# Gate and up products of the latent tokens as seven half-size products (Strassen's algorithm) in a two-layer diffusion trunk

## The chip, the core and the metric

One core of a Trainium2 chip runs the whole kernel in one launch. The metric is the device time of an execution in microseconds, as the median of several runs.

## What is computed

The reference is a trunk of two layers over 1024 latent tokens and 256 context tokens of width 1024, in float32. Each layer has a mixer (gated linear attention, spatial gating, windowed attention, one output projection) and a SwiGLU feed-forward block, both between norms and with modulation:

```
y = concat(a, b, c) @ w_out                     # mixer output
x = x + mod[2] * rmsnorm(y, n1_post)
h = modulate(rmsnorm(x, n2_pre), mod[3], mod[4])
g, u = split(h @ w_gu, 2)                       # w_gu 1024 x 5632
f = (silu(g) * u) @ w_down                      # w_down 2816 x 1024
x = x + mod[5] * rmsnorm(f, n2_post)
```

The last layer computes the feed-forward block for the latent tokens alone. The modulation vectors are `silu(c) @ mod_w + mod_b`, six of 1024 for each layer and each of the two streams of tokens.

## The kernel before, in words

Tokens stand in ten tiles of 128: tiles 0 and 1 are context, 2 to 9 latent. Every matrix product is done with both operands split into a high part (a cast to fp32r) and a low part, the rest. `mm3` (L179) issues three matmuls for one product: high x high, high x low, low x high. A split of something that lies in SBUF is a cast on ScalarE and a subtraction on VectorE; `split` (L164) does this for a weight: a load by SP into one of two staging tiles `ws`, the cast (L172), the subtraction (L173).

`ffn` (L1096) runs everything after the mixer of a layer. It goes over the tokens in two halves, `HALVES`: five tiles each in layer 0, four each in layer 1. For each half the output projection runs first: `cat_tile` transposes the mixer's output, and `down_group` (L972, matmuls at L984) multiplies a tile by four weight slices at a time, with pairs of 512-column matmuls into two PSUM banks, and collects the sums in `yas`. `post` (L1001) norms, gates and adds the residual; `normed` and `modulate` (L403, transposes at L400) make the transposed input of the feed-forward block, split into `hh` and `hl`.

Then, per half, the 22 chunks of 128 hidden units. `ahead` splits the gate and up weights of a chunk before they are needed. `product` (L1151) computes for a chunk and a stretch of tokens the gate and the up product, each over 8 slices of 128 of the model's width and each with three matmuls; ScalarE takes SiLU of the gate out of PSUM, VectorE multiplies by the up product, and the result is split into `gh` and `gl`. In layer 0 a half of 640 tokens is done in two stretches of 320 columns (384 and 256 in the first group), in layer 1 a half is one stretch of 512. After every four chunks `down_group` adds their part of the down-projection to `yas`. All weights of gate, up and down are therefore loaded and split once for each half.

In layer 0 a second generator, `mod_stream` with "dve", is merged with `ffn`: seven pieces of modulation vectors, each 16 loads of 128x512 into a ring `ms` of two tiles, and for each load two VectorE operations (L376 for the first of a sum, L378 for the rest) that add a row of the weights times a scalar into `macc`. `merge` takes from each generator in proportion to its planned total (here 840 units for `ffn`, 105 for the sums), and the order in which the program text is recorded is, with a scheduler's look-ahead, the order on each engine.

Of the kernel before, what the change touches and what calls it, by code (L numbers as in the profile page):

```python
# [16 lines left out]
D = 1024  # L17
# [104 lines left out]

class Net:
# [55 lines left out]
    def mm3(self, out, ah, al, bh, bl, first, last):  # L179
        mm = self.nc.tensor.matmul  # L180
        mm(out, ah, bh, start=first, stop=False)  # L181
        mm(out, ah, bl, start=False, stop=False)  # L182
        mm(out, al, bh, start=False, stop=last)  # L183
# [859 lines left out]
    def layer(self, l):  # L1043
# [3 lines left out]
        with tp("ss", "left") as sp_:  # L1047
# [41 lines left out]
        with tp("ff", "left") as fp:  # L1089
            streams = [(420.0 * (2 if need_ctx else 1.6), self.ffn(l, fp, need_ctx))]  # L1090
            if l + 1 < self.layers:
                streams.append((MOD_SHARE_FFN, self.mod_stream("dve", [(0, 5)] + [(l + 1, j) for j in (1, 0, 2, 3, 4, 5)])))
                self.mring = fp, 2
            merge(*streams)

    def ffn(self, l, fp, need_ctx):  # L1096
        nc, a = self.nc, self.a
        halves = [list(range(*x)) for x in (HALVES if need_ctx else ((CT, 6), (6, TT)))]
        G = 4
        hh, hl = self.H  # L1100
        WO, WG, WD = a["w_out"], a["ffn_w_gu"], a["ffn_w_down"]
        row = lambda w, k: w[l, k * P : (k + 1) * P, :]
        seconds = dict(tags=("dh", "dl"), pool=fp)

        def cat_tile(slot, i):
            pv = self.turned(self.cat[i], None)
            s = slice(slot * P, (slot + 1) * P)
            nc.scalar.copy(hh[:, :, s], pv)
            nc.vector.tensor_sub(hl[:, :, s], pv, hh[:, :, s].bitcast(F32))

        def cats(tiles):
            return [lambda slot=slot, i=i: cat_tile(slot, i) for slot, i in enumerate(tiles)]

        queue = [c for _ in halves for c in range(NFC)]
        ready = []

        def ahead():
            if queue:
                c = queue.pop(0)
                ready.append([self.split(self.cols(WG, l, 0, KC, f * FF + c * P, f * FF + (c + 1) * P), D) for f in range(2)])  # L1120

        early = cats(halves[0])
        for f in early[:2]:
            f()
        with self.tc.high_priority(offset=400):
            w0 = [self.split(row(WO, k), D) for k in range(4)]
        for f in early[2:]:
            f()
        w1 = [self.split(row(WO, k), D, **seconds) for k in range(4, 8)]
        gates = self.gates(l, 2, fp, need_ctx)  # L1130
        yas = [self.t(fp, f"ya{t_}", [P, D]) for t_ in range(5)]
        norm2 = [self.normed(2 * l + 1, lambda i: self.x1[l][i], tiles, l, 3) for tiles in halves]
        for hi, tiles in enumerate(halves):
            done = lambda ti, i: self.post(fp, i, yas[ti], gates, self.x_src(l, i), self.x1[l][i], self.ss[2 * l + 1], False, not need_ctx)
            yield from self.down_group([hh[:, k, :] for k in range(4)], [hl[:, k, :] for k in range(4)], w0, tiles, yas, True, None, None)
            if hi == 0:
                w0 = [self.split(row(WO, k), D) for k in range(4)]
            else:
                ahead()
            yield from self.down_group([hh[:, k, :] for k in range(4, 8)], [hl[:, k, :] for k in range(4, 8)], w1, tiles, yas, False, done,  # L1140
                                       cats(halves[1]) if hi == 0 else norm2[0])
            if hi == 0:
                w1 = [self.split(row(WO, k), D, **seconds) for k in range(4, 8)]
        groups = [range(0, NFC % G)] + [range(c, c + G) for c in range(NFC % G, NFC, G)]
        final = l == self.layers - 1
        for hi, tiles in enumerate(halves):
            n = len(tiles) * P
            for gi, cs in enumerate(groups):
                ghs, gls, wts = [], [], []

                def product(pair, ci, p0, p1):  # L1151
                    s, sz = slice(p0, p1), p1 - p0
                    ps = self.b2()
                    for wi, (wh, wl) in enumerate(pair):
                        for k in range(KC):
                            ks = slice(k * P, (k + 1) * P)
                            self.mm3(ps[:, wi * 512 : wi * 512 + sz], wh[:, ks], wl[:, ks], hh[:, k, s], hl[:, k, s], k == 0, k == KC - 1)
                    sg = self.t(fp, "sg", [P, 512], bufs=2)[:, :sz]
                    self.act(sg, ps[:, :sz], AF.Silu)
                    nc.vector.tensor_mul(sg, sg, ps[:, 512 : 512 + sz])  # L1160
                    nc.scalar.copy(ghs[ci][:, s], sg)
                    nc.vector.tensor_sub(gls[ci][:, s], sg, ghs[ci][:, s].bitcast(F32))
                    return 6.5 * sz / 320

                def begin():
                    pair = ready.pop(0)
                    for x, o in (("gh", ghs), ("gl", gls)):
                        o.append(self.t(fp, x, [P, 640], F32R, bufs=5))
                    return pair

                if gi == 0:

                    pairs = [begin()]
                    ahead()
                    pairs.append(begin())
                    for ci in range(2):
                        yield product(pairs[ci], ci, 0, n - 256)
                    wts.append(self.split(row(WD, cs[0]), D, **seconds))
                    yield product(pairs[0], 0, n - 256, n)
                    ahead()  # L1180
                    wts.append(self.split(row(WD, cs[1]), D, **seconds))
                    yield product(pairs[1], 1, n - 256, n)
                else:
                    parts = 2 if n > 512 else 1
                    for ci, c in enumerate(cs):
                        pair = begin()
                        ahead()
                        for p_ in range(parts):
                            yield product(pair, ci, p_ * n // parts, (p_ + 1) * n // parts)
# [146 lines left out]
```

## Time and profile before

| | |
|---|---|
| median of 3 runs | 2998.67 us (2994.62 to 3002.09) |
| profiled execution, its own time | 2993.22 us |
| its span | 2991.4 us |
| mean granted clock of TensorE | 0.978 |
| feed-forward part of layer 0, from the out-projection's first matmul to the last of the down-projection | 627.0 to 1688.2 us |
| the same of layer 1, to the end of the span | 2156.5 to 2991.4 us |

The profile is that of one execution. Busy time is the time in which an engine worked on an instruction; matmuls overlap their neighbours, so that the mean length of one is more than the distance from one start to the next, and their ends are modelled. Times in the timeline are counted from the span's start.

### The profile page before, as it was taken

Reading aid. Unit: us, or ns where it says so; the run is one execution under the profiler, and the core shown is the slowest. Engines: PE = TensorE matmul, PEld = TensorE weight load, DVE = VectorE, ACT = ScalarE, POOL = GpSimd, SP = SyncE. Lnnn points to the kernel's source line nnn. Section 1 sums busy time; section 2 is a strip of 40 time slices with the busy share of each in tenths; the row PEclk is TensorE's granted clock in tenths of the full one; section 3 lists DMA queues with packets and bytes.
Section 4 is the critical chain, followed back from the end, with each engine's and each line's share of the span. In section 5 each row is a group of like instructions: output and inputs, shape, how many; then the busy total and the mean of one; then the engine's idle time right before and its main releaser. Section 6 shows DMA issues by size and latency. Waiting matters only on the chain. (4 is left out here: it accounts for less than half of the span.)

```text
span 2991.4 us, 45447 instructions
## 1 busy us (share of the span) xinstructions
PE 2883.5 (96%) x18072; PEld 2570.9 (86%) x18072; DVE 1750.9 (59%) x3586; ACT 1220.2 (41%) x2426; POOL 209.2 (7%) x172
## 2 busy tenths in 40 slices
PE   6999899989999999999999999899799999999998
PEld 4899788878999999999999899888688888888887
DVE  3465577878866533885333685688776333553334
ACT  4453576644422222522222464577554222342222
POOL 0000233300000000000000000233200000000000
PEclk8999799989999999999999999999899999999999
DMA  8743000076644322553222453100465332353232
GB/s 242 216 142 90 24 12 8 22 245 204 198 131 152 106 85 83 182 166 106 85 71 73 126 147 92 57 9 12 140 212 170 101 102 87 101 160 101 89 92 78
DMA packets 347393, 338.05 MB, mean 113 GB/s; under 512 B 42528, under 2 KB 284460, under 8 KB 347180
## 3 DMA queue, kind: packets, MB, share of 16 engines
q1 hardware_dynamic: 344924, 329.37, 36.0%
q0 software_dynamic: 1536, 3.15, 0.4%
q8 instruction: 142, 2.33, 0.3%
q10 hardware_dynamic: 720, 2.62, 0.2%
q14 instruction: 71, 0.58, 0.1%
HBM read 304.38 MB, written 30.70 MB: 112 GB/s over the span
## 5 line engine op out<-in xcount | busy, mean ns | idle before, releaser
L181 PE MATMUL b<-hh,wh 128*128 128x320 f32 (+3 forms) x2648 | 870.9, 329 | 4.2 <-DVE ht L411 3.0
L182 PE MATMUL b<-hl,wh 128*128 128x320 f32 (+3 forms) x2648 | 868.2, 328 | 0.0
L183 PE MATMUL b<-hh,wl 128*128 128x320 f32 (+3 forms) x2648 | 868.0, 328 | 0.0
L181 PEld LDWEIGHTS b<-hh,wh 128*128 128x128 f32 x2648 | 498.4, 188 | 35.3 <-DVE ht L411 3.9
L182 PEld LDWEIGHTS b<-hl,wh 128*128 128x128 f32 x2648 | 498.3, 188 | 26.6 <-issue 0.8
L183 PEld LDWEIGHTS b<-hh,wl 128*128 128x128 f32 x2648 | 498.3, 188 | 25.3
L173 DVE TENSOR_TENSOR wl<-ws,wh 128x1024 fp32r<-128x1024 f32 x192 | 234.6, 1224 | 412.1 <-ACT wh L172 411.8
L172 ACT CAST wh<-ws 128x1024 fp32r<-128x1024 f32 x192 | 201.2, 1050 | 475.0 <-PE b L182 352.1
L172 ACT CAST dh<-ws 128x1024 fp32r<-128x1024 f32 x104 | 108.9, 1047 | 348.1 <-PE b L984 270.3
L984 PE MATMUL b<-dh,gh 128*128 128x512 f32 x792 | 246.2, 391 | 0.2 <-ACT ya L989 0.2
L984 PE MATMUL b<-dl,gh 128*128 128x512 f32 x792 | 244.9, 390 | 0.5 <-DVE dl L173 0.5
L991 DVE TENSOR_TENSOR ya<-ya,b 128x512 f32<-128x512 f32 x216 | 139.5, 682 | 180.9 <-PE b L984 180.8
L984 PE MATMUL b<-dh,gl 128*128 128x512 f32 x792 | 244.6, 390 | 0.0
L181 PE MATMUL b<-wh,hh 128*128 128x256 f32 (+1 forms) x592 | 173.2, 294 | 8.2 <-DVE hh L413 3.8
L984 PEld LDWEIGHTS b<-dl,gh 128*128 128x128 f32 x792 | 148.5, 188 | 32.4 <-DVE dl L173 1.6
L984 PEld LDWEIGHTS b<-dh,gl 128*128 128x128 f32 x792 | 148.7, 188 | 31.2
L984 PEld LDWEIGHTS b<-dh,gh 128*128 128x128 f32 x792 | 147.1, 188 | 30.5 <-ACT ya L989 0.9
L183 PE MATMUL b<-wh,hl 128*128 128x256 f32 (+1 forms) x592 | 171.0, 289 | 1.2 <-DVE hl L414 1.2
L182 PE MATMUL b<-wl,hh 128*128 128x256 f32 (+1 forms) x592 | 171.5, 290 | 0.3 <-DVE wl L487 0.3
L487 DVE TENSOR_TENSOR wl<-ws,wh 128x1024 fp32r<-128x1024 f32 (+2 forms) x68 | 79.8, 1176 | 152.7 <-ACT wh L486 152.7
L173 DVE TENSOR_TENSOR dl<-ws,dh 128x1024 fp32r<-128x1024 f32 x104 | 127.1, 1222 | 62.9 <-ACT dh L172 62.4
L378 DVE SCALAR_TENSOR_TENSOR macc<-ms,csil,macc 128x512 f32<-128x512 f32 x196 | 139.5, 746 | 37.0 <-DMA ms<-in_mod_w 36.5
(257 smaller groups left out, 4682.3 us busy)
## 6 DMA issues: line engine op xcount, KB each, us to landing
ws<-in_ffn_w_gu SPq DMA_DIRECT2D x176, 512.0 KB, 3.9
ws<-in_ffn_w_down SPq DMA_DIRECT2D x88, 512.0 KB, 3.6
ms<-in_mod_w SPq DMA_DIRECT2D x144, 256.0 KB, 3.0
ws<-in_w_in SPq DMA_DIRECT2D x56, 512.0 KB, 4.3
ws<-in_w_out SPq DMA_DIRECT2D x32, 512.0 KB, 4.6
xt<-cat SPq DMA_DIRECT2D x18, 512.0 KB, 4.6
xt<-x SPq DMA_DIRECT2D x18, 512.0 KB, 3.6
xp<-x SPq DMA_DIRECT2D x18, 512.0 KB, 4.7
```

The source lines that it names most:

```text
L172: nc.scalar.copy(h[:, :width], sv)
L173: nc.vector.tensor_sub(l[:, :width], sv, h[:, :width].bitcast(F32))
L181: mm(out, ah, bh, start=first, stop=False)
L182: mm(out, ah, bl, start=False, stop=False)
L183: mm(out, al, bh, start=False, stop=last)
L378: nc.vector.scalar_tensor_tensor(x, st, c, x, op0=ALU.mult, op1=ALU.add)
L487: nc.vector.tensor_sub(lo[:, : kk * nn], st[:, : kk * nn], h[:, : kk * nn].bitcast(F32))
L984: nc.tensor.matmul(ps[n], x[:, s], y[:, n * 512 : (n + 1) * 512], start=(c == 0 and pi == 0), stop=(c == nk - 1 and pi == 2))
L991: nc.vector.tensor_add(y, y, ps[n])
```

## The change

The gate and up product of the latent tokens is a product of a 1024 x 1024 activation matrix with, for each chunk, a 1024 x 256 weight matrix (128 gate columns and 128 up columns). The new class `Up` cuts it in two by two blocks: tokens 2 to 5 and 6 to 9 (`a1.`, `a2.`), first and second half of the width (`a.1`, `a.2`; `b1.`, `b2.`), gate and up (`b.1`, `b.2`). In place of eight block products it does seven, of 4 slices x 3 matmuls x 512 columns each, of sums of blocks: `t1` to `t4` are made of the weights, `s1` to `s4` of the activations. A chunk now serves all latent tokens at once. GpSimd computes the four weight differences of a chunk (`diff`) and the two products of gate and up; ScalarE copies three partial results out of PSUM and VectorE makes three sums that read PSUM; seven weight blocks are split per chunk (`prepare`, by `halve`), each 128x512, into slots that exist once. The results go to DRAM (`gd`, DMAs issued by GpSimd).

Around it the stages are laid out anew. `mix_out` does the output projection of all tiles with all eight weight slices resident, post and norm one and two tiles behind, and the sums of activations (VectorE and GpSimd; `s3`, `s4` and `a22` through DRAM); the norm's root goes by table. Then the stream of chunks, in layer 0 merged with the modulation sums (418 to 105 units). `up_context` then computes gate and up of the 256 context tokens with ordinary products, for which it loads `w_gu` a second time. `down_stage` runs the down-projection as before with `down_group`, from activations re-read from DRAM and split again; the down weights are still loaded once for each half.

```diff
+class Up:
+    DIFFS = {"t1": ("b12", "b11"), "t2": ("b22", "t1"), "t3": ("b22", "b12"), "t4": ("b21", "t2")}
...
+    def load(self, c):
+        for f in range(2):
+            t = self.stage(f).rearrange("p (k n) -> p k n", k=KC)
+            self.nc.sync.dma_start(t, self.net.cols(self.net.a["ffn_w_gu"], self.l, 0, KC, f * FF + c * P, f * FF + (c + 1) * P))
+            self.raw[c, f"b1{f + 1}"], self.raw[c, f"b2{f + 1}"] = t[:, 0:4], t[:, 4:8]
...
+    def diff(self, c, x):
+        p, q = self.DIFFS[x]
+        v = self.raw[c, x] = self.net.t(self.gp, "tt", [P, 4, P], bufs=3)
+        self.nc.gpsimd.tensor_sub(v, self.raw[c, p], self.raw[c, q])
+
+    def prepare(self, c, x):
+        self.net.halve(*self.slot(c, x), self.raw[c, x])
...
+    def chunk(self, c):
+        nc, net, n = self.nc, self.net, c + 1
+        more = n < NFC
+        xz, Y = net.b2(), net.b1()
+        X, Z = xz[:, :512], xz[:, 512:]
+        store = lambda at, t: nc.gpsimd.dma_start(self.gd[c][:, at : at + 512], t)
+        self.product(X, c, "b11", "a11", True)
+        p1 = self.tmp()
+        nc.scalar.copy(p1, X)
+        self.product(Y, c, "b21", "a12", True)
+        g0 = self.tmp()
+        nc.vector.tensor_add(g0, Y, p1)
+        net.act(g0, g0, AF.Silu)
+        yield 5.4
+        if more:
+            self.load(n)
+        self.product(X, c, "t2", "s2")
+        u2 = self.tmp()
+        nc.scalar.copy(u2, X)
+        self.product(Z, c, "t1", "s1", True)
+        p5 = self.tmp()
+        nc.scalar.copy(p5, Z)
+        if more:
+            self.prepare(n, "b11")
+            self.prepare(n, "b21")
+            self.diff(n, "t1")
+            self.diff(n, "t2")
+        yield 5.4
+        self.product(X, c, "t3", "s3")
+        c22 = self.tmp()
+        nc.vector.tensor_add(c22, X, p5)
+        if more:
+            self.prepare(n, "t1")
+            self.prepare(n, "t2")
+        yield 2.7
+        self.product(Z, c, "b22", "s4")
+        c12 = self.tmp()
+        nc.vector.tensor_add(c12, Z, u2)
+        nc.gpsimd.tensor_mul(g0, g0, c12)
+        store(256, g0)
+        if more:
+            self.diff(n, "t3")
+            self.prepare(n, "b22")
+            self.prepare(n, "t3")
+        yield 2.7
+        self.product(X, c, "t4", "a22")
+        g1 = self.tmp()
+        net.act(g1, X, AF.Silu)
+        nc.gpsimd.tensor_mul(g1, g1, c22)
+        store(768, g1)
+        if more:
+            self.diff(n, "t4")
+            self.prepare(n, "t4")
+        yield 2.7
...
+            with tp("cx", "left") as cx:
+                streams = [(NFC * 19.0, st)]
+                if l + 1 < self.layers:
+                    streams.append((MOD_SHARE_FFN, self.mod_stream("dve", [(0, 5)] + [(l + 1, j) for j in (1, 0, 2, 3, 4, 5)])))
+                    self.mring = cx, 2
+                merge(*streams)
...
+    def mix_out(self, l, px, A, up, tp):
...
+        for n, i in enumerate(order):
+            product(i)
+            if n + 2 < len(order):
+                cat(order[n + 2])
+            if n:
+                post(order[n - 1])
+                residual(i)
+            if n > 1:
+                norm(order[n - 2])
+            if n == len(order) - 3:
+                up.load(0)
+                up.prepare(0, "b11")
+                up.prepare(0, "b21")
...
+    def halve(self, h, lo, v):
+
+        self.nc.scalar.copy(h, v)
+        self.nc.vector.tensor_sub(lo, v, h.bitcast(F32))
```

Three places show how instructions stand now. On GpSimd, behind the last work of layer 0's mixer, there was nothing until the mixer of layer 1 (`ao`, `cat` and `sink` belong to the mixers, `uv` to layer 1's):

```order
L827 TENSOR_TENSOR ao_7017<-v_484,gld_7014 128x256 [waits DMAHW3_49,DMAHW5_49,DVE_49,Pool_49]
L827 TENSOR_TENSOR ao_7023<-v_484,gld_7020 128x256 [waits DMAHW4_49,DMAHW6_49,DVE_49,Pool_49]
L950 DMA cat_84<-co_6358 128x512 [waits DVE_49]
L1261 TENSOR_SCALAR sink_16687<-sink_16687 128x8 [waits DMAHW6_49,DVE_49,PE_49]
L1248 DMA uv_18596<-in_gdi 128x2x512 [waits DMAHW0_49,DMASW2_49,DMAHW1_49,DMASW1_49,DMAHW2_49,DMASW0_49,DMAHW3_49,DVE_49,DMAHW7_49,PE_49,Activation_49]
```

Now a chunk of the stream puts six operations and two stores there (`ct` are the temporaries of `chunk`, `tt` the differences t1, t2, t3, t4 in this order, `ru` and `rg` the loaded weights of up and gate):

```order
L230 TENSOR_TENSOR ct_9086<-ct_9086,ct_9190 128x512 [waits DVE_49]
L197 DMA gd_0_7114<-ct_9086 128x512 [waits DMASW2_49,Pool_49]
L240 TENSOR_TENSOR ct_9216<-ct_9216,ct_9155 128x512 [waits DMASW1_49,Activation_49]
L173 TENSOR_TENSOR tt_9305<-ru_9267,rg_9265 128x512 [waits DMAHW4_49,DMAHW0_49]
L197 DMA gd_0_7114<-ct_9216 128x512 [waits Pool_49]
L173 TENSOR_TENSOR tt_9307<-ru_9267,tt_9305 128x512 [waits Pool_49]
L173 TENSOR_TENSOR tt_9363<-ru_9267 128x512 [waits DVE_49]
L173 TENSOR_TENSOR tt_9389<-rg_9265,tt_9307 128x512 [waits DVE_49,Pool_49]
```

The first difference of a chunk stands behind the last product of the chunk before, and the last difference frees `rg` for its next load.

On VectorE, in layer 0's feed-forward part, the sums (`macc`) stood between halvings of weights and of results:

```order
L378 SCALAR_TENSOR_TENSOR macc_10416<-ms_10727,csil_150,macc_10416 128x512 [waits DMAHW2_49,DVE_49]
L378 SCALAR_TENSOR_TENSOR macc_10416<-ms_10727,csil_150,macc_10416 128x512 [waits DVE_49]
L173 TENSOR_TENSOR wl_9587<-ws_9584,wh_9586 128x1024 [waits PE_49,Activation_49]
L378 SCALAR_TENSOR_TENSOR macc_10416<-ms_10759,csil_150,macc_10416 128x512 [waits DMAHW3_49,DVE_49]
L378 SCALAR_TENSOR_TENSOR macc_10416<-ms_10759,csil_150,macc_10416 128x512 [waits DVE_49]
L378 SCALAR_TENSOR_TENSOR macc_10416<-ms_10819,csil_150,macc_10416 128x512 [waits DMAHW4_49,DVE_49]
L1160 TENSOR_TENSOR sg_9567<-sg_9567,b_1665_9518 128x320 [waits Activation_49]
L173 TENSOR_TENSOR wl_9593<-ws_9590,wh_9592 128x1024 [waits DMAHW5_49]
L1162 TENSOR_TENSOR gl_9443<-sg_9567,gh_9442 128x320 [waits Activation_49]
```

Now they stand between the halvings of the seven blocks (`t1l` is not shown, `t3l`, `b11l`, `b21l`, `b22l` are) and the sums L222 and L229 that empty PSUM:

```order
L503 SCALAR_TENSOR_TENSOR macc_10037<-ms_10173,csil_150,macc_10037 128x512 [waits DMAHW2_49,DVE_49]
L503 SCALAR_TENSOR_TENSOR macc_10037<-ms_10173,csil_150,macc_10037 128x512 [waits DVE_49]
L503 SCALAR_TENSOR_TENSOR macc_10037<-ms_10181,csil_150,macc_10037 128x512 [waits DMAHW3_49,DVE_49]
L503 SCALAR_TENSOR_TENSOR macc_10037<-ms_10181,csil_150,macc_10037 128x512 [waits DVE_49]
L222 TENSOR_TENSOR ct_9677<-b_1801_9578,ct_9647 128x512 [waits PE_49,Activation_49]
L1384 TENSOR_TENSOR t3l_9714<-tt_9707,t3h_9713 128x512 [waits Activation_49]
L1384 TENSOR_TENSOR b11l_9820<-rg_9787,b11h_9819 128x512 [waits DMAHW4_49,Activation_49]
L1384 TENSOR_TENSOR b21l_9824<-rg_9787,b21h_9823 128x512 [waits PE_49,Activation_49]
L503 SCALAR_TENSOR_TENSOR macc_10037<-ms_10233,csil_150,macc_10037 128x512 [waits DMAHW5_49,DVE_49]
L503 SCALAR_TENSOR_TENSOR macc_10037<-ms_10233,csil_150,macc_10037 128x512 [waits DVE_49]
L229 TENSOR_TENSOR ct_9703<-b_1801_9578,ct_9633 128x512 [waits DMASW4_49,PE_49]
L1384 TENSOR_TENSOR b22l_9710<-ru_9619,b22h_9709 128x512 [waits Activation_49]
```

The two sums that read PSUM wait for TensorE and stand in one row with everything else; the halving of `b21` of a chunk two ahead stands before the sum L229.

On TensorE, at the end of a chunk (`b_1801` holds its X and Z, `b_1875` the Y of the chunk two ahead), this is the row; before, all matmuls of a chunk and a stretch stood together:

```order
L305 MATMUL b_1801_9578<-s4h_8426,b22l_9541 128x512
L305 MATMUL b_1875_9918<-a12h_7105,b21h_9823 128x512 [waits Activation_49]
L305 MATMUL b_1875_9918<-a12l_7106,b21h_9823 128x512
L305 MATMUL b_1875_9918<-a12h_7105,b21l_9824 128x512 [waits DVE_49]
L305 MATMUL b_1875_9918<-a12h_7105,b21h_9823 128x512
L305 MATMUL b_1875_9918<-a12l_7106,b21h_9823 128x512
L305 MATMUL b_1875_9918<-a12h_7105,b21l_9824 128x512
L305 MATMUL b_1875_9918<-a12h_7105,b21h_9823 128x512
L305 MATMUL b_1801_9578<-a22h_8428,t4h_9570 128x512 [waits DVE_49]
L305 MATMUL b_1801_9578<-a22l_8429,t4h_9570 128x512
```

The second product of the chunk two ahead (with `b21h`, `b21l`) begins in front of the chunk's last product (with `t4h`), and the latter waits for VectorE's sum L222.

## Rows read from the trace of the kernel before

**Rows 1.** The page's first part: busy time, share of the span, instructions of each engine.
```profile
PE 2883.5 (96%) x18072; PEld 2570.9 (86%) x18072; DVE 1750.9 (59%) x3586; ACT 1220.2 (41%) x2426; POOL 209.2 (7%) x172
```

**Rows 2.** Busy time by stretch: length, engines with instructions, clock, DMA share, GB/s.
```profile
680.00:720.00 40.00, 38.86 (x177) 31.55 (x176) 36.06 (x91) 22.37 (x35) 0.00 (x0) 1.00 0.76 256
1200.00:1400.00 200.00, 200.00 (x1232) 189.00 (x1231) 156.76 (x283) 70.32 (x124) 0.00 (x0) 1.00 0.52 163
2400.00:2600.00 200.00, 200.00 (x888) 165.54 (x886) 75.60 (x88) 50.98 (x61) 0.00 (x0) 1.00 0.33 98
```

**Rows 3.** TensorE's timeline, three places: start, length, instruction; 320, 512 and 256 columns.
```profile
999.88 0.31 PE L181 MATMUL b<-hh,wh 128*128 128x320 f32 x1
...
1002.08 0.31 PE L181 MATMUL b<-hh,wh 128*128 128x320 f32 x1
...
2420.80 0.39 PE L181 MATMUL b<-hh,wh 128*128 128x512 f32 x1
...
2425.33 0.39 PE L183 MATMUL b<-hh,wl 128*128 128x512 f32 x1
...
250.10 0.28 PE L181 MATMUL b<-wh,hh 128*128 128x256 f32 x1
...
253.94 0.28 PE L183 MATMUL b<-wh,hl 128*128 128x256 f32 x1
```

**Rows 4.** TensorE's timeline, layer 0's gate and up product begins; idle before in brackets.
```profile
753.02 0.44 PE L181 MATMUL b<-hh,wh 128*128 128x384 f32 x1 [2.29 <-DVE ht L411]
...
756.45 0.48 PE L183 MATMUL b<-hh,wl 128*128 128x384 f32 x1
756.77 0.34 PE L181 MATMUL b<-hh,wh 128*128 128x384 f32 x1
756.94 0.33 PE L182 MATMUL b<-hl,wh 128*128 128x384 f32 x1
```

**Rows 5.** SP's timeline, the out-projection's weights in layer 0.
```profile
628.43 1.47 SPq L169 DMA_DIRECT2D ws<-in_w_out  x2
...
635.16 2.83 SPq L169 DMA_DIRECT2D ws<-in_w_out  x2
```

**Rows 6.** Groups by form: line, engine, operation, count, busy us, mean ns, idle before.
```profile
L173 DVE TENSOR_TENSOR wl<-ws,wh 128x1024 fp32r<-128x1024 f32 x192 | 234.6, 1224 | 412.1 <-ACT wh L172 411.8
L172 ACT CAST wh<-ws 128x1024 fp32r<-128x1024 f32 x192 | 201.2, 1050 | 475.0 <-PE b L182 352.1 <-DMA ws<-in_ffn_w_gu 96.4 <-DMA ws<-in_w_out 21.1
...
L378 DVE SCALAR_TENSOR_TENSOR macc<-ms,csil,macc 128x512 f32<-128x512 f32 x196 | 139.5, 746 | 37.0 <-DMA ms<-in_mod_w 36.5
...
L1162 DVE TENSOR_TENSOR gl<-sg,gh 128x512 fp32r<-128x512 f32 x40 | 27.5, 686 | 7.6 <-ACT gh L1161 7.6
...
L154 ACT ACTIVATE sg<-b 128x512 f32<-128x512 f32 x40 | 23.5, 588 | 13.0 <-PE b L183 13.0
```

**Rows 7.** The page's DMA issues: count, KB each, median us from issue to landing.
```profile
ws<-in_ffn_w_gu SPq DMA_DIRECT2D x176, 512.0 KB, 3.9
```

**Rows 8.** Timelines of VectorE and GpSimd in layer 0's mixer, 404 to 416.
```profile
406.63 0.69 DVE L909 TENSOR_TENSOR ptl<-b,pth 128x512 fp32r<-128x512 f32 x1 [1.40 <-ACT pth L908]
...
405.64 2.37 POOL L737 TENSOR_TENSOR qk<-qk,ep 128x1024 f32<-128x1024 f32 x1 [12.70 <-ACT ep L154]
...
411.46 1.28 POOL L749 TENSOR_TENSOR lv<-el,k 128x512 f32<-128x512 f32 x1 [1.12 <-ACT el L154]
```

**Rows 9.** VectorE's timeline in layer 0's feed-forward stage: two neighbours.
```profile
1254.39 0.74 DVE L378 SCALAR_TENSOR_TENSOR macc<-ms,csil,macc 128x512 f32<-128x512 f32 x1
1255.05 1.22 DVE L173 TENSOR_TENSOR wl<-ws,wh 128x1024 fp32r<-128x1024 f32 x1
```

**Rows 10.** Timelines of VectorE and GpSimd in layer 0's mixer, 338 to 350.
```profile
340.70 3.73 DVE L862 TENSOR_TENSOR qs<-sq,qs 64x512 fp32r<-64x512 f32 x2
...
340.09 2.12 POOL L734 TENSOR_TENSOR qk<-q,k 128x1024 f32<-128x1024 f32 x1 [2.32 <-PE b L757]
342.17 1.71 POOL L749 TENSOR_TENSOR lv<-el,k 128x512 f32<-128x512 f32 x1
```

More of the change, by code (lines that the diff above doesn't have):

```diff
@@ L177, in cols, with mm3 @@
         return w[l, k0 * P : k1 * P, c0:c1].rearrange("(k p) n -> p k n", p=P)
[L179 to L183, printed above, removed]
+    def mm3(self, out, ah, al, bh, bl, first, last, more=False):
+        mm = lambda x, y, **kw: self.nc.tensor.matmul(out, x, y, skip_group_check=more, **kw)
+        mm(ah, bh, start=first, stop=False)
+        mm(ah, bl, start=False, stop=False)
+        mm(al, bh, start=False, stop=last)
     def rstd(self, ss, n, scale, eps, out=None):
@@ L1087, in layer @@
                 merge(*streams)
-        self.open_hp()
[L1089 to L1096, printed above, removed]
+        with tp("fa", "left") as fa:
+            A = {x + p: self.t(fa, x + p, [P, 4, 512], F32R) for x in ("a11", "a12", "s2", "s1") for p in "hl"}
+            up = Up(self, l, fa, A)
+            with tp("px", "left") as px:
+                rest = self.mix_out(l, px, A, up, tp)
+                next(rest)
+                st = up.stream()
+                next(st)
+                for _ in rest:
+                    pass
+            with tp("cx", "left") as cx:
[4 more added lines that the diff above has]
+                merge(*streams)
+            up.close()
@@ L1111, in cats @@
[L1111 to L1123, printed above, removed]
-            f()
-        with self.tc.high_priority(offset=400):
-            w0 = [self.split(row(WO, k), D) for k in range(4)]
@@ L1127, in ffn @@
[L1127 to L1189, printed above, removed]
-                        wts.append(self.split(row(WD, c), D, **seconds))
-                last = gi == len(groups) - 1
-                nxt = None
-                if last and hi + 1 < len(halves):
-                    nxt = norm2[hi + 1]
-                elif last and not final:
-                    nxt = self.normed(2 * l + 2, lambda i: self.x_src(l + 1, i), range(5), l + 1, 0)
-                    self.plan(l + 1)
-                if last and hi == 0:
-                    gates = self.gates(l, 5, fp, need_ctx)
-                done = lambda ti, i: self.post(fp, i, yas[ti], gates, self.x1[l][i], self.x_dst(l, i),
-                                               self.ss[2 * l + 2] if need_ctx else None, final and hi == 1, not need_ctx)
-                yield from self.down_group(ghs, gls, wts, tiles, yas, gi == 0, done if last else None, nxt)
@@ new lines, in down_stage, with fetch @@
+        sizes = [[2, 4, 4, 4, 4, 4], [4, 3, 3, 3, 3, 3, 3]]
+        work = []
+        for hi in range(2):
+            c = 0
+            for n in sizes[hi]:
+                work.append((hi, range(c, c + n)))
+                c += n
+        def fetch():
+            if not work:
+                return None
+            hi, cs = work.pop(0)
+            g, w = [], []
+            for c in cs:
+                w.append(weight(c))
+                g.append(acts(c, halves[hi]))
+            loads[0] += 1
+            return hi, cs, g, w
@@ new lines, in down_stage @@
+        cur = fetch()
+        yas = [self.t(dn, f"ya{t_}", [P, D]) for t_ in range(5)]
+        gates = self.gates(l, 5, dn, need_ctx)
+        nxt = []
+        if not final:
+            nxt = self.normed(2 * l + 2, lambda i: self.x_src(l + 1, i), range(5), l + 1, 0)
+        while cur:
+            ahead = fetch()
+            hi, cs, g, w = cur
+            tiles = halves[hi]
+            last = cs.stop == NFC
+            done = lambda ti, i: self.post(dn, i, yas[ti], gates, self.x1[l][i], self.x_dst(l, i),
+                                           self.ss[2 * l + 2] if need_ctx else None, final and hi == 1, not need_ctx)
+            for _ in self.down_group([x for x, _ in g], [x for _, x in g], w, tiles, yas, cs.start == 0, done if last else None, None):
+                pass
+            if hi == 1 and cs.start and nxt:
+                nxt.pop(0)()
+                if len(nxt) == 1:
+                    self.plan(l + 1)
+            cur = ahead
@@ L1204, in x_dst @@
+        for f in nxt:
+            f()
     def x_dst(self, l, i):
```

215 lines of the change are left out of this document (205 added, 10 removed).

## The prediction

> **What bounds the kernel now.** I read the page's first part, then busy time by stretch, then start times on TensorE, then its waits. TensorE is busy for 2883.5 of 2991.4 us [rows 1]. In the feed-forward stretches it has no hole: 200.00 of 200 us from 1200 to 1400 and from 2400 to 2600, at granted clock 1.00, that is 2.4 GHz, while the DMA share is 0.52 and 0.33 [rows 2]. So each matmul less there is worth its start-to-start time, not its busy time, which overlaps the next one's. These steps are 0.1467 us for 320 columns (15 of them from 999.88 to 1002.08), 0.2265 for 512 (20 from 2420.80) and 0.120 for 256 (32 from 250.10) [rows 3]. VectorE is busy 157 and 76 us of 200 in these stretches, GpSimd not at all [rows 2]: the change takes its time from engines that seem to have room, and for each I ask whether the room is enough.
>
> **What is removed.** Layer 0: 22 chunks x 2 matrices x 8 slices x 3 products = 1056 groups, each 4 matmuls of 320 columns on average over the two halves, so 4224 x 0.1467 = 619.7 us. After: 22 x 7 products x 12 = 1848 matmuls of 512 columns, 418.6 us, and for the 256 context tokens, which keep eight products, 1056 of 256 columns, 126.7 us: 74.4 us less. Layer 1: 2112 x 0.2265 = 478.4 us become 418.6: 59.8 us less. Out-projection and down-projection keep their columns. Together **-134.2 us**. The old stages lose little that could be won back: from 680 to 720 TensorE misses 1.1 us [rows 2]; at 753.02 it waits 2.29 us for the normed tile, then the 384-column matmuls start 0.32 us apart until 756.5, then 0.17, as at 1.2 and 2.4 GHz, which costs another 1.6 [rows 4]. With as much for layer 1, I give **-8 us**.
>
> **What is added outside the stream.**
> - Out-projection. A tile now needs all eight weight slices, through two staging tiles; pairs were issued 6.7 us apart (628.43, 635.16) [rows 5], so the last comes some 20 us after the first, and a tile is 48 matmuls or 10.9 us plus transposes. Tiles 0 and 1 interleave as slices arrive, so I take **+6** (0 to 12).
> - Post and norm per tile. VectorE has the gating, the residual, the splits, each like the 1.22 us of a 128x1024 operation [rows 6], and small steps: about 10 us under 12.9 us of TensorE (10.9 and 16 transposes). Eighteen tiles, GpSimd joining for the sums of four: **+14** (0 to 40).
> - Turn to the stream. In layer 1 nothing stands between the last norm and chunk 0; s3, s4 and a22 go to DRAM and back (two transfers of about 3.9 us, as a weight load [rows 7]), and chunk 1's load waits for chunk 0's differences. In layer 0 the context tiles cover this. **+18** for both (8 to 35).
> - Context part: first load, cast and subtraction, 3.9 + 1.05 + 1.22 us [rows 6, 7], and a slow start of the clock as in [rows 4]: **+8** (4 to 12). Then 1 MB of weights per 48 x 0.120 = 5.8 us is 182 GB/s, with the stores some 210; 256 GB/s were moved at share 0.76 with TensorE at 38.86 of 40 us [rows 2], so **+5** (0 to 20).
> - Down stages: each must refill weights and re-split activations: **+12** (6 to 20).
>
> **The stream of chunks.** Its price decides. TensorE needs 84 x 0.2265 = 19.03 us per chunk. GpSimd gets six 128x512 operations (four differences, two products), 1.28 us each [rows 8]: 7.7 us. ScalarE has twelve at 0.6 us [rows 6], 7.2; VectorE ten, of which seven halve (0.69 us [rows 6]; 0.61 with the overlap that two sums show in [rows 9]) and three read PSUM. In layer 1 that fits. A loop remains there: product with a22, SiLU 0.59, five GpSimd operations 6.4, weight load 3.9, two casts 1.24, one subtraction 0.69, then 7 + 12 matmuls 4.3, in all 17.1, with hand-overs about 18, under 19.03. **+6** (0 to 20).
>
> In layer 0 the modulation sums of the next layer run beside it, six loads a chunk for about 18.7 of 22 chunks (112 loads), each two VectorE operations of 0.746 us [rows 6], 0.66 start to start [rows 9]. In the old stage GpSimd was silent. Where both worked at once, in the mixer, they did not overlap: while GpSimd ran 2.12 and 1.71 us from 340.09, two VectorE operations with both inputs in SBUF took 3.73 us from 340.70, where such an operation alone takes about 0.69 [rows 6, 10]. A VectorE operation that reads one input from PSUM kept its 0.69 us under a GpSimd operation of 2.37 us [rows 8]. So GpSimd's 7.7 us, seven halvings (4.3) and twelve sums (8.0) stand one behind the other: 20.0 us, already over TensorE's 19.03. That is the lower bound. If VectorE's other work (three PSUM additions 1.8, transposes and reductions of the sums 1.8 per chunk) never falls under GpSimd's, it is 23.6. I take 22.0, near the middle, since VectorE executes in order and only some of that work will coincide: 18.7 x 2.97 = **+56 us** (18 to 86).
>
> The Trainium skill ("SBUF — State Buffer", section "SBUF: two separate sides") calls the ports of the two engines an exclusive lock: a VectorE operation with two SBUF inputs and a GpSimd operation that reads SBUF shut each other out for a whole instruction. The trace agrees: 3.73 us for what takes 1.4 alone. By that rule alone the stream costs 20.0 us a chunk and the term is +18; without it, by engine loads alone, 0.
>
> **Sum:** -134.2 - 8 + 6 + 14 + 18 + 8 + 5 + 12 + 6 + 56 = -17 against the profiled execution of 2993.2, so 2976. That execution lies 5.5 us under the median 2998.7; carried over, **2982 us**, 0.6% less. About 0.3%, 9 us, is what a measurement of this kernel can tell from no change. By the bounds of the stream's term the forecast has 2944 to 3012.
>
> **Rivals.**
> - *Slower: VectorE and GpSimd in series, and TensorE waits each time.* Place: layer 0's stream. TensorE executes in order, with the second product of a chunk two ahead in front of the product with a22; its b21 needs a weight load that stands on SP's queue behind modulation loads, which wait for VectorE. If each GpSimd operation also waits half a VectorE operation (6 x 0.35 us), a chunk grows from 23.6 to 25.7 us, and a wait over 2 us can bring 3.5 us at half rate [rows 4]. Price 18.7 x 6.7 = 125 in place of 56: 3051 us. It turns the sign above about 23 us a chunk. For it: [rows 10]; against: TensorE stands two chunks ahead.
> - *Faster: the waits stay hidden.* VectorE was busy 157 of 200 us with the same sums and TensorE lost nothing [rows 2]. If the sums lag and are made up at the end of the stream and in the context part, a chunk costs about 19.3 us, 5 us in all: 2982 - 51 = 2931.
> - *The turns are dearer than taken.* Mixing at +40, turns at +35, and layer 1's loop 15% longer (20.7 us, +37): 26 + 17 + 31 more gives 3056, half of it 3019. In layer 1 no context tiles cover the turn.
> - *The half-size products do not keep 0.2265 us.* They are the same form as the old ones [rows 3], so I give this almost nothing. At 2% more it is 2 x 418.6 x 0.02 = 17: 2999.
>
> **How the numbers follow.** Forecast 0.46 (about 0.27 of it faster, 0.12 same, 0.07 slower); hidden 0.20, faster; series 0.22 and dear turns 0.10, slower; slow products 0.02, same. So faster 0.47, same 0.14, slower 0.39. The range takes in the hidden case with some room below and the series case at its centre: 2920 to 3055; the forecast's own is 2944 to 3012.
>
> **What would show it.** Right: 512-column starts 0.2265 us apart in both streams; a chunk every 22 us in layer 0's while modulation loads arrive and every 19 to 20 after them and in layer 1; TensorE's waits there naming VectorE's c22 and c12 or ScalarE's cast of b21; VectorE's two-input operations with means well above 0.69 us in that stretch and GpSimd's above 1.28. Wrong: a chunk every 19.1 us in layer 0 (the hidden case), or 25 and more, with granted clock below 1.00 (series); or gaps of tens of us at the turns.

## The result and the profile after

The change makes the kernel slower: 3136.8 us as the median of 4 runs (3134.0 to 3139.6) against 2996.6 (2994.2 to 3002.1), a ratio of 1.0465 with a 95% interval of 1.0446 to 1.0484. The forecast was 2982 us, 0.6% less, and the range ended at 3055.

TensorE's busy time fell by only 33 us, at a granted clock of 0.962 on average against 0.978, and the span grew: the page's first part, to be set beside [rows 1].

```profile
PE 2850.4 (91%) x16296; PEld 2367.7 (76%) x16296; DVE 1897.3 (61%) x3632; ACT 1332.4 (43%) x2748; POOL 659.0 (21%) x562
```

Where TensorE has holes now is seen in busy time by stretch (columns as in [rows 2]): the turn to layer 0's stream of chunks, nine chunks beside the modulation sums, three chunks of the same stream in which none were due, the context part, and layer 1's stream.

```profile
753.00:804.00 51.00, 33.66 (x129) 24.32 (x127) 33.37 (x49) 31.19 (x58) 15.17 (x11) 0.87 0.52 176
...
832.00:1067.00 235.00, 194.24 (x774) 146.50 (x775) 207.90 (x264) 61.45 (x109) 86.80 (x72) 0.95 0.46 140
1089.00:1154.30 65.30, 61.82 (x263) 45.79 (x261) 22.52 (x37) 20.63 (x37) 27.42 (x24) 1.00 0.25 73
...
1341.00:1468.00 127.00, 123.41 (x1026) 122.94 (x1024) 62.60 (x71) 54.24 (x72) 11.93 (x22) 1.00 0.74 210
...
2430.00:2840.00 410.00, 387.91 (x1592) 287.96 (x1591) 131.70 (x190) 128.42 (x226) 173.73 (x152) 1.00 0.23 74
```

The context part is full, at 210 GB/s. The streams are not: 194 of 235 us with the sums, and 388 of 410 even in layer 1, where nothing runs beside them. How much is lost shows in the distance from one chunk's product with t4 to the next one's. In layer 1 that is 21.65 us nearly every time, where 84 x 0.2265 would be 19.03; in layer 0 it is 21.4 to 21.7 without the sums (19.7 for the last) and 23.7 to 28.5 with them. Over the 21 steps of a layer:

```
                     layer 0   layer 1    (84 x 0.2265 x 21 = 399.5)
the change            517.0     453.3
```

That is 117 us lost in layer 0 and 54 in layer 1. The list of TensorE's waits names who (total us, times, longest); the first two come once a chunk:

```profile
PE b L305 <- DVE ct L222: 48.0, 41, 4.3
PE b L305 <- ACT ct L210: 47.8, 43, 2.0
PE b L1109 <- ACT dh L1383: 15.9, 3, 9.9
...
PE b L305 <- DVE z L1297: 14.2, 1, 14.2
...
PE b L305 <- ACT ch L1383: 9.2, 1, 9.2
```

One chunk of layer 1 in the timeline (start, length, instruction, idle before in brackets), of TensorE, then ScalarE, then GpSimd:

```profile
2539.85 0.50 PE L305 MATMUL b<-a22h,t4h 128*128 128x512 f32 x1
...
2547.04 0.39 PE L305 MATMUL b<-s2h,t2l 128*128 128x512 f32 x1
...
2548.17 0.39 PE L305 MATMUL b<-a11h,b11h 128*128 128x512 f32 x1
2549.53 0.50 PE L305 MATMUL b<-s1h,t1h 128*128 128x512 f32 x1 [0.97 <-ACT ct L210]
2549.87 0.39 PE L305 MATMUL b<-s1l,t1h 128*128 128x512 f32 x1
...
2557.44 0.50 PE L305 MATMUL b<-s4h,b22h 128*128 128x512 f32 x1 [0.16 <-DVE ct L222]
...
2561.50 0.50 PE L305 MATMUL b<-a22h,t4h 128*128 128x512 f32 x1
...
2548.37 0.62 ACT L1383 CAST t2h<-tt 128x512 fp32r<-128x512 f32 x1 [2.66 <-POOL tt L173]
2548.90 0.58 ACT L210 COPY ct<-b 128x512 f32<-128x512 f32 x1
...
2547.04 1.30 POOL L173 TENSOR_TENSOR tt<-ru,tt 128x512 f32<-128x512 f32 x1
```

The product s1 x t1 writes Z, yet it waits for L210, the copy that reads X; s4 x b22 writes Z and waits for L222, which reads X. X and Z are the two halves of one PSUM tile, and the wait stands between them. L210 in turn is late here because it stands on ScalarE behind the cast of t2h, which waits for a GpSimd difference that ends at 2548.34. A matmul that has waited also starts its successor 0.34 us later in place of 0.2265 (2549.53 to 2549.87), and there are several in a chunk.

Beside the sums, in layer 0, VectorE and GpSimd stop each other, as [rows 10] had it; VectorE, GpSimd and TensorE in one chunk:

```profile
862.36 4.25 DVE L503 SCALAR_TENSOR_TENSOR macc<-ms,csil,macc 128x512 f32<-128x512 f32 x2
...
861.25 1.75 POOL L173 TENSOR_TENSOR tt<-ru,rg 128x512 f32<-128x512 f32 x1
...
863.54 1.30 POOL L173 TENSOR_TENSOR tt<-ru,tt 128x512 f32<-128x512 f32 x1
864.78 1.27 POOL L173 TENSOR_TENSOR tt<-ru 128x512 f32<-128x512 f32 x1
...
873.01 3.15 DVE L503 SCALAR_TENSOR_TENSOR macc<-ms,csil,macc 128x512 f32<-128x512 f32 x4 [0.82 <-DMA ms<-in_mod_w]
876.09 0.68 DVE L222 TENSOR_TENSOR ct<-b,ct 128x512 f32<-128x512 f32 x1
...
876.82 0.50 PE L305 MATMUL b<-s4h,b22h 128*128 128x512 f32 x1 [2.58 <-DVE ct L222]
```

Two sums that take 1.4 us alone take 4.25 while the differences run. Later in the chunk TensorE waits 2.58 us for the sum L222, which stands on VectorE behind four more sums; how much of those 2.58 us the exclusion made can't be read from this place alone. As groups by form, the sums have gone from 746 ns [rows 6] to 954:

```profile
L503 DVE SCALAR_TENSOR_TENSOR macc<-ms,csil,macc 128x512 f32<-128x512 f32 x196 | 178.1, 954 | 18.3 <-DMA ms<-in_mod_w 17.8
...
L501 DVE TENSOR_SCALAR macc<-ms,csil 128x512 f32<-128x512 f32 x28 | 30.3, 1123 | 3.0 <-DMA ms<-in_mod_w 3.0
```

The nine chunks hold a third loss, beside the tile and the exclusion. Behind most of its longest waits TensorE runs for some 3 us at half its clock (three rows of TensorE; then a stretch, columns as in [rows 2]):

```profile
1062.04 0.50 PE L305 MATMUL b<-s4h,b22h 128*128 128x512 f32 x1 [4.29 <-DVE ct L222]
...
1063.08 0.63 PE L305 MATMUL b<-s4l,b22h 128*128 128x512 f32 x1
1063.50 0.63 PE L305 MATMUL b<-s4h,b22l 128*128 128x512 f32 x1
```

```profile
1063.10:1066.40 3.30, 3.30 (x9) 2.61 (x8) 2.62 (x4) 0.86 (x3) 0.00 (x0) 0.50 0.16 60
```

The granted clock there is 0.50, that is 1.2 GHz, and starts are 0.43 us apart. In layer 0's 21 steps some 83 starts stand so, which is 17 us more than at 0.2265; layer 1's steps have no such stretch.

Last, the turn to layer 1's stream (TensorE; one row of ScalarE):

```profile
2351.00 0.62 PE L1279 MATMUL b<-oh,cl 128*128 128x512 f32 x2
...
2372.99 0.77 PE L305 MATMUL b<-a11h,b11h 128*128 128x512 f32 x1 [14.16 <-DVE z L1297]
...
2386.82 0.50 PE L305 MATMUL b<-s2h,t2h 128*128 128x512 f32 x1 [4.06 <-ACT s2h L1383]
...
2362.02 1.02 ACT L348 ACTIVATE z<-b 128x1024 f32<-128x1024 f32 x1
```

From the last matmul of the out-projection to chunk 0's product with t4 (2409.4) it is 58.4 us, in layer 0 (752.0 to 804.3) 52.3, for some 22 us of matmuls and transposes each. Chunk 1 waits for the PSUM tile of the last out-projection, whose post begins on ScalarE 11 us after the last matmul.

### The profile page after: what moved, and what is told of

Read it like the earlier page. It is cut to its first block, busy times and chain, and to the rows that moved or that the text cites. A ratio compares the mean times of both kernels' runs of the same rounds, so it can differ in the third digit from the quotient of the medians.

```text
span 3133.5 us, 43693 instructions
## 1 busy us (share of the span) xinstructions
PE 2850.4 (91%) x16296; PEld 2367.7 (76%) x16296; DVE 1897.3 (61%) x3632; ACT 1332.4 (43%) x2748; POOL 659.0 (21%) x562
## 4 chain that ended last, share of the span: by engine, by line
PE 58%; DVE 16%; DMA 9%; ACT 6%; issue 6%; POOL 4%; SPq 1%; DVEq 0%; ACTq 0%; POOLq 0%
PE b L305 25%; PE b L1109 17%; DVE macc L503 3%; PE b L1279 3%; DMA ms<-in_mod_w 3%; POOL tt L173 3%; PE b L1010 2%; PE b L1028 2%; PE b L1045 2%; DMA ru<-in_w_out 1%; DMA rg<-in_ffn_w_gu 1%; PE b L882 1%; PE b L894 1%; DVE macc L501 1%; DVE ct L222 1%
## 5 line engine op out<-in xcount | busy, mean ns | idle before, releaser
L1109 PE MATMUL b<-dh,g 128*128 128x512 f32 x828 | 227.8, 394 | 15.9 <-ACT dh L1383 15.9
L1109 PE MATMUL b<-wh,g 128*128 128x512 f32 x756 | 209.3, 396 | 0.0
L1109 PEld LDWEIGHTS b<-dh,g 128*128 128x128 f32 x828 | 157.5, 191 | 49.8 <-ACT dh L1383 16.8
L1109 PEld LDWEIGHTS b<-wh,g 128*128 128x128 f32 x756 | 141.9, 188 | 34.4 <-ACT ya L1114 0.3
L305 PE MATMUL b<-hh,wh 128*128 128x320 f32 (+1 forms) x472 | 148.8, 315 | 0.0
L305 PE MATMUL b<-hl,wh 128*128 128x320 f32 (+1 forms) x472 | 147.2, 312 | 0.0
L305 PE MATMUL b<-hh,wl 128*128 128x320 f32 (+1 forms) x472 | 146.8, 311 | 0.0
L1109 PE MATMUL b<-dl,g 128*128 128x512 f32 x414 | 129.9, 395 | 0.6 <-DVE dl L1384 0.5
L611 ACT CAST wh<-ws 128x1024 fp32r<-128x1024 f32 (+2 forms) x68 | 68.6, 1012 | 134.2 <-PE b L305 81.0
L305 PEld LDWEIGHTS b<-wh,hh 128*128 128x128 f32 x592 | 114.3, 193 | 11.8 <-issue 5.5
L1109 PE MATMUL b<-wl,g 128*128 128x512 f32 x378 | 118.7, 395 | 0.0
```

Source lines behind the costliest of these rows:

```text
L305: mm = lambda x, y, **kw: self.nc.tensor.matmul(out, x, y, skip_group_check=more, **kw)
L611: nc.scalar.copy(h[:, : kk * nn], st[:, : kk * nn])
L1109: nc.tensor.matmul(ps[n], x[:, s], y[:, n * 512 : (n + 1) * 512], start=(c == 0 and pi == 0), stop=(c == nk - 1 and pi == 2))
```

## The experiments

Theory A: a chunk loses 2.6 us because X and Z share a tile. Its rival B: the loop through GpSimd's differences, the weight load and the casts, put at 18 us in the prediction, really takes 21.65. Theory C: layer 0's extra 5 us are VectorE and GpSimd shutting each other out; its rival D: weight loads wait on SP's queue behind modulation loads. Theory E: the turns are long because the last post stands behind chunk 0's weight preparation.

**split_xz.**

```diff
-        xz, Y = net.b2(), net.b1()
-        X, Z = xz[:, :512], xz[:, 512:]
+        X, Z, Y = net.b1(), net.b1(), net.b2()[:, :512]
```

> X and Z, the two running sums of a chunk, get a PSUM tile each in place of two halves of one tile; Y takes half of a double tile. Theory A (TensorE waits in every chunk because a matmul into one half waits until the other half is read out): layer 1's chunks go from 21.65 us to 19.1 to 19.8, layer 0's undisturbed ones too, the waits naming the copy L210 and the sum L222 (48 us each) fall below 10, and the kernel wins 80 to 110 us: 3030 to 3055 us. Rival B (the loop through GpSimd's differences, the weight load and the cast sets 21.65 us): the chunks stay at 21.6, the waits only change their names, time within 15 us of 3137.

Measured: 3046.6 us (3039.5 to 3048.2), ratio to the kernel before 1.0145 (1.0123 to 1.0166): 90 us less than the change. Layer 1's chunks come every 19.3 us, and in the stretch from 2392 to 2776 one wait of 2.8 us is all that is left of TensorE's waits:

```profile
2507.03 0.39 PE L304 MATMUL b<-a22h,t4h 128*128 128x512 f32 x1
...
2526.30 0.39 PE L304 MATMUL b<-a22h,t4h 128*128 128x512 f32 x1
```

```profile
PE b L304 <- DVE ct L221: 2.8, 1, 2.8
```

Rival B falls as it was put: the GpSimd operations, the load and the casts are all still there, and fit into 19.3 us. The wait of s1 x t1 for ScalarE is gone, and the products of two chunks are no longer interleaved; they stand whole, one behind the other, so that between a product and the one that needs its read-out there is another of 2.7 us. Both came of the one edit, so what the tile and what the order gave is not told apart. In layer 0 the chunks beside the sums still take 20 to 27 us.

**no_gpsimd.**

```diff
-        v = self.raw[c, x] = self.net.t(self.gp, "tt", [P, 4, P], bufs=3)
-        self.nc.gpsimd.tensor_sub(v, self.raw[c, p], self.raw[c, q])
+        self.raw[c, x] = self.raw[c, p]
...
-        nc.gpsimd.tensor_mul(g0, g0, c12)
...
-        nc.gpsimd.tensor_mul(g1, g1, c22)
```

> The four weight differences and the two products of gate and up are left out of every chunk (the seven blocks split are raw weight blocks, gate is stored without up); VectorE's and ScalarE's work is as before. Rival B: layer 1's chunks fall from 21.65 to about 19.1 us. Theory A: layer 1's stay above 21 us. For layer 0's extra 5 us beside the modulation sums: if it is GpSimd and VectorE shutting each other out (theory C), its chunks fall from about 26.5 us to 22 to 23 and the sums' mean from 954 ns to about 750; if it is the queue of SP, where weight loads stand behind modulation loads (theory D), they stay above 25 us.

Measured in a single run: 3080.4 us. Layer 1's chunks alternate between 20.3 and 22.7 us, 21.7 on average. By what was expected this speaks for A, but the average is the same for another reason; TensorE's waits in twelve of these chunks (2430 to 2700) are

```profile
PE b L302 <- ACT b11h L1380: 8.9, 6, 1.6
PE b L302 <- ACT ct L209: 6.1, 6, 1.0
```

The copy L209 (L210 of the change) still holds up s1 x t1 once in two chunks, with no GpSimd operation left. In the other chunk TensorE waits for the cast of b11, whose weight load comes later here. So this run is no second proof against B; split_xz has to bear that alone. Layer 0's chunks come every 20.1 to 24.8 us, 22.1 on average, with the same loads through the same ring, which speaks against theory D. The ring also empties sooner when the sums are quick, so the trace of the change has to settle it. The whole list of TensorE's waits in the nine chunks from 832 to 1067 is

```profile
PE b L305 <- DVE ct L222: 26.8, 9, 4.3
PE b L305 <- ACT ct L210: 12.7, 9, 2.0
PE b L305 <- DVE ct L229: 1.1, 4, 0.3
PE b L305 <- ACT b21h L1383: 0.2, 1, 0.2
```

Only the last, 0.2 us, is for a freshly loaded weight block, so D as it was put is out. A smaller thing stands beside C there: VectorE, with L222 in its row, waits 13.2 us in these chunks for the loads of the sums themselves. The sums are back at their old mean:

```profile
L500 DVE SCALAR_TENSOR_TENSOR macc<-ms,csil,macc 128x512 f32<-128x512 f32 x196 | 138.2, 747 | 22.4 <-DMA ms<-in_mod_w 21.8
```

**narrow_sums.**

```diff
-                        nc.vector.scalar_tensor_tensor(x, st, c, x, op0=ALU.mult, op1=ALU.add)
+                        nc.vector.scalar_tensor_tensor(x[:, :64], st[:, :64], c, x[:, :64], op0=ALU.mult, op1=ALU.add)
```

> The modulation sums (all but the first of each) work on 64 columns in place of 512, so the modulation vectors are not the reference's; loads, order and waits stay. Theory C: VectorE's side of the exclusion shrinks by about 7 us a chunk, layer 0's chunks fall from 26.5 us to about 21.7, GpSimd's six operations come near 1.3 us each; the kernel wins some 70 to 80 us. Theory D: the loads still pass the ring of two tiles one by one, 6 loads of 3 us through two tiles, so the chunks stay above 24 us.

Measured in a single run: 3106.5 us, 30 less than the change, where 70 to 80 were expected. Sums an eighth as wide still last 492 ns on average:

```profile
L503 DVE SCALAR_TENSOR_TENSOR macc<-ms,csil,macc 128x64 f32<-128x64 f32 x196 | 88.3, 492 | 47.8 <-DMA ms<-in_mod_w 46.7
```

So my reckoning of theory C was too simple: narrowing the sums takes away their own length but not the waits. Four of them took 3.73 us while GpSimd made its differences (its last ends at 862.38), two took 0.48 when it was silent:

```profile
858.93 3.73 DVE L503 SCALAR_TENSOR_TENSOR macc<-ms,csil,macc 128x64 f32<-128x64 f32 x4 [1.08 <-DMA ms<-in_mod_w]
...
865.45 0.48 DVE L503 SCALAR_TENSOR_TENSOR macc<-ms,csil,macc 128x64 f32<-128x64 f32 x2 [1.39 <-DMA ms<-in_mod_w]
```

Everything behind them on VectorE stands as long. Layer 0's chunks beside the sums stay at 22 to 26 us. Alone this run would have spoken as much for D.

**post_first.**

```diff
+        post(order[-1])
+        norm(order[-2])
         wo_cm.__exit__(None, None, None)
         up.open(tp)
...
         yield
-        post(order[-1])
-        norm(order[-2])
         norm(order[-1])
```

> The last tile's post and the last norm but one are recorded before chunk 0's weight differences and splits, not behind them. If the turn to the stream is long because the last post stands behind the weight preparation on ScalarE and VectorE (theory E), the 14.2 us wait for z (L1297) in layer 1 falls below 5 and the stretch from the out-projection's last matmul to chunk 0's last product (58 us in layer 1, 52 in layer 0) shortens by 8 to 14 us in each layer: 3115 to 3122 us. If it is the way of s3, s4 and a22 through DRAM, the wait moves to s2h to s4h and the time stays within 8 us of 3137.

Measured in a single run: 3153.0 us, 16 more. The wait for z is gone and another has its place, TensorE's for b11 of chunk 1, whose cast waits for a load that came late (TensorE, then ScalarE):

```profile
2387.21 0.80 PE L305 MATMUL b<-a11h,b11h 128*128 128x512 f32 x1 [11.37 <-ACT b11h L1383]
...
2386.54 0.62 ACT L1383 CAST b11h<-rg 128x512 fp32r<-128x512 f32 x1 [0.79 <-DMA rg<-in_ffn_w_gu]
```

The turn of layer 1 is as long as before, 58.3 us (2364.1 to 2422.4). Theory E falls. That the posts, norms and weight preparations are each other's delay, whichever is first, fits both runs and is not shown.

**vector_only**, then, is the opposite test of theory C: the work stays, on the engine that has less room.

```diff
-        self.nc.gpsimd.tensor_sub(v, self.raw[c, p], self.raw[c, q])
+        self.nc.vector.tensor_sub(v, self.raw[c, p], self.raw[c, q])
...
-        nc.gpsimd.tensor_mul(g0, g0, c12)
+        nc.vector.tensor_mul(g0, g0, c12)
...
-        nc.gpsimd.tensor_mul(g1, g1, c22)
+        nc.vector.tensor_mul(g1, g1, c22)
```

> The change as it is, with its six GpSimd operations per chunk (four differences, two products) given to VectorE; X and Z share their tile as before. If GpSimd's and VectorE's operations shut each other out (theory C), the exchange is free: 6 x 0.61 = 3.7 us on VectorE in place of 7.7 us in which VectorE stood still. Layer 0's chunks beside the modulation sums go from 26.5 to 22 to 23.5 us, the sums' mean back to 0.75 us, layer 1's chunks stay at 21.6, and the time falls by 40 to 70 us, to 3067 to 3097. If the engines work side by side and VectorE is simply full (rival), VectorE gets 3.7 us more a chunk and layer 0's chunks grow to 27 or more: 3140 to 3170.

Measured in a single run: 3036.5 us, 100 less than the change, more than expected, with six operations a chunk more on VectorE. The sums last 745 ns:

```profile
L503 DVE SCALAR_TENSOR_TENSOR macc<-ms,csil,macc 128x512 f32<-128x512 f32 x196 | 139.9, 745 | 3.4 <-DMA ms<-in_mod_w 3.4
```

Layer 0's chunks take 19.9 to 22.4 us in all but the ends. Layer 1's fell as well, from 21.65 to 20.3, which I had not expected. In place of GpSimd's difference the cast of t2h here waits for the end of s2 x t2 (one row of TensorE, two of ScalarE):

```profile
2547.99 0.39 PE L305 MATMUL b<-s2h,t2l 128*128 128x512 f32 x1
...
2548.19 0.62 ACT L1383 CAST t2h<-tt 128x512 fp32r<-128x512 f32 x1 [1.30 <-PE b L305]
2548.71 0.58 ACT L210 COPY ct<-b 128x512 f32<-128x512 f32 x1
```

The copy L210 begins 0.72 us after the start of the last matmul of s2 x t2, in the change 1.86 us after it (2547.04, 2548.90), and a chunk lies 1.3 us over 19.03 where it had been 2.6. So half of what the change loses in layer 1 needs both, the shared tile and a GpSimd that is late.

**split_vector** joins both edits; it was run twice, the second time beside the next kernel but one.

> Separate tiles for X and Z and all six operations on VectorE. By theories A and C together layer 1's chunks are 19.3 us, layer 0's beside the sums 19.5 to 21.5 (VectorE's own load is 13 x 0.61 + 3 x 0.6 + 12 x 0.67 = 17.8 us and some 1.8 for the sums' transposes, 19.6), so about 18 x 3.5 us less than with separate tiles alone (3047): 2975 to 3000 us, level with or a little under the kernel before. By the rival (VectorE full) 3050 or more.

Measured: 2985.1 us (2981.8 to 2990.9), ratio to the kernel before 0.9944 (0.9926 to 0.9963).

> The same kernel as split_vector, timed again beside the next one: 2980 to 2992 us; the question is whether it is under the kernel before by more than 0.3%.

Measured: 2984.6 us, 0.9946 (0.9931 to 0.9962). Layer 1's chunks stand 19.3 us apart, layer 0's 19.3 to 21.7, and in layer 0's stream VectorE is now busy 352 of 388 us, with TensorE at 379.5 and full clock:

```profile
830.00:1218.00 388.00, 379.53 (x1666) 303.71 (x1666) 351.74 (x573) 131.82 (x234) 20.97 (x38) 1.00 0.51 151
```

**split_vector_spread** takes some of VectorE's sums out of the stream.

```diff
+                    mods = self.mod_stream("dve", [(0, 5)] + [(l + 1, j) for j in (1, 0, 2, 3, 4, 5)])
+                    streams.append((88.0, mods))
...
+                merge(*streams, until=st)
...
+                        merge((NFC * 6.0, self.up_context(l, cu, up)), (26.0, mods))
```

> As split_vector, and the modulation sums are spread: four loads in each chunk of layer 0's stream in place of six, the rest beside the context's gate and up. VectorE's load per chunk falls to about 17 us, under TensorE's 19.0, and all of layer 0's chunks should come at 19.3 to 20 us: 10 to 25 us less than split_vector, 2955 to 2985. If layer 0's chunks stay above 21 us, something other than VectorE's load holds them (the way of the weights through SP's queue behind modulation loads).

Measured: 2989.2 us (2988.2 to 2990.1), 0.9962 (0.9947 to 0.9977). The steps of layer 0 went from 413.4 to 412.3 us, nothing, though VectorE was busy 353 us in them and not 372, and the wait for the context's first cast grew from 10.6 to 17.9 us. So VectorE's load no longer set the pace. Layer 0's steps still lie 16 us above layer 1's; what holds those was not tried.

**sums_on_vector** gives VectorE the last of GpSimd's arithmetic in these stages.

```diff
-            nc.gpsimd.tensor_sub(a21, a11, a21)
+            nc.vector.tensor_sub(a21, a11, a21)
...
-            nc.gpsimd.tensor_sub(a12, a12, a11)
+            nc.vector.tensor_sub(a12, a12, a11)
```

> split_vector with the two activation sums that GpSimd still makes per tile (L1334, L1336 of the change's numbering; eight in each layer) on VectorE too, so that GpSimd only issues stores. If part of the turn to the stream is GpSimd and VectorE shutting each other out in the chain of the last norms (some 2 us a tile and layer), each turn shortens by 3 to 6 us: 6 to 12 us less than split_vector. If the turn is the chain of norm, sums, splits and transposes itself, within 4 us of it.

Measured: 2977.1 us (2973.7 to 2978.1), 0.9919 of the kernel before (0.9905 to 0.9933), 7.5 less than split_vector beside it. The turns went from 54.7 to 46.6 us and from 55.3 to 51.7. This kernel beats both.

All kernels, 21 steps from chunk to chunk in each layer, from the starts on TensorE's timeline:

```
                     layer 0   layer 1   time
the change            517.0     453.3    3136.8
split_xz              473.6     402.9    3046.6
no_gpsimd             464.8     455.2    3080.4
narrow_sums           486.1     454.6    3106.5
post_first            522.7     455.6    3153.0
vector_only           440.3     426.9    3036.5
split_vector          413.4     396.1    2985.1
split_vector_spread   412.3     396.4    2989.2
sums_on_vector        411.9     395.6    2977.1
```

The last rows lie about 399.5 because the first two steps are short: TensorE has then done part of the next chunk already.

## Why the prediction was wrong, by its steps

- **The matmuls removed, -134.2 us: right, but for some 11 us.** In split_vector a chunk of layer 1 is 19.27 us without a wait: its 84 starts stand 0.2294 us apart on average, 1.3% over 0.2265, which is 11 us over 44 chunks. The rival of slow half-size products was priced at 2%; why they are slower at all is open.
- **Layer 1's stream, +6 (0 to 20): wrong, and it was 54.** This is the step that failed. I followed the loop through GpSimd and the weight load and found 18 us under 19.03; that loop, as a whole, did not bind. I did not follow the read-outs of PSUM, although the order shows X and Z under one name. split_xz shows it: 50 of the 54 us gone with the tile divided and the order that came with it. GpSimd's row did reach TensorE by a way that I had not drawn, through the cast of t2h and the copy L210 behind it: with GpSimd silent and the tile still shared (vector_only) 26 of the 54 us are gone.
- **Layer 0's stream, +56 (18 to 86): mechanism right, too small, and it was 117.** Three things are in the 61 us. The forecast had no shared tile: dividing it alone takes 43 us off layer 0's steps, giving GpSimd's work to VectorE alone 77, both 104, so the two overlap. It had no half clock, which costs the change 17 us here; in vector_only the granted clock from 830 to 1218 is 1.00. And it sized the exclusion for six loads a chunk over 18.7 chunks, where the trace has 142 sums in nine chunks, eight loads, in 14 of the steps, and none in the others. By the prediction's own method that is 7.7 + 4.3 + 15.8 x 0.67 = 22.6 us at the least and 26.2 with nothing of VectorE's other work under GpSimd's. Measured are 26.25 on average in the 14 steps. That this meets the far bound is luck in part: the bound is that of a VectorE with no idle time, and in these nine chunks it was busy 208 of 235 us, while tile and clock, which the bound leaves out, have their share.
- **The rivals.** *Series* had the right place, the half clock behind the waits and nearly the right price for layer 0 (25.7 us a chunk; 3051), and it missed layer 1. It had 0.22; the lock that the trace shows in [rows 10] deserved more. *Dear turns* had two of its places right and both too small (turns 35 against 66, layer 1's loop 37 against 54), and the mixing that it feared did not come.
- **The turns, +18 (8 to 35): mis-sized.** Against some 22 us of TensorE's work each they lost about 30 in layer 0 and 36 in layer 1, 66 in all. I counted on context tiles to cover layer 0's, and took the chain of post, norm, sums and splits as idle engines would run it. Part was the exclusion again: with GpSimd's two sums a tile on VectorE the turns fell by 8 and 4 us. What the chain would take without weight preparation beside it was not tried.
- **Out-projection, post and norm; context; down stages:** within their bounds. From 625 to 753, layer 0's out-projection, TensorE is busy 126 of 128 us; the context's first matmul waits 9.2 us against +8 taken, and 210 GB/s passed beside a TensorE at 123.4 of 127; the down stages wait 2.8, 3.2 and 9.9 us for their first weights, against +12.

The three misses, 61 + 48 + 48 us, are the 155 us between 2982 and 3137, to 2 us. The other terms were not measured one by one and the matmuls missed by 11, so that close a fit is chance.

## What to carry to other kernels

Where a product waits for a read-out, look at which tile the wait is on: here two running sums in one PSUM tile made neighbours wait for each other, and the matmul-bound stream paid for it in every round. Work moved to an idle GpSimd wasn't free while VectorE read two SBUF operands beside it; count both engines as one row, and where VectorE is the faster, as here with 0.69 us against 1.28, leave the work there. And a sum of engine loads prices one engine in series; what TensorE loses by waiting on it, half clock included, is a term of its own.

## What the runs showed that I had not expected

An operation with one tensor from SBUF and one scalar a partition was held up as well: the first sum of each, a multiplication by that scalar, went from 479 to 1123 ns (L501 above), where the kernel before had

```profile
L376 DVE TENSOR_SCALAR macc<-ms,csil 128x512 f32<-128x512 f32 x28 | 12.6, 479 | 4.4 <-DMA ms<-in_mod_w 4.4
```

The Trainium skill ("SBUF — State Buffer", section "SBUF: two separate sides") names, beside operations with two SBUF inputs, those in a mode that uses two ports; that this one is such an operation is not shown here, but 1123 against 479 ns agrees with it. And the width of the shut-out operation hardly changed its wait: sums of 64 columns took 492 ns on average where two alone took 0.48 us, some 250 more for each, and sums of 512 columns 954 where they take 746, some 210 more.
